# First stage of a hybrid layer on one core: loads reordered, c spread over all rows, squares and sums on four engines, sets that begin with 1, 2, 3 and 3 tiles of K

## The chip, the cores and the metric

The kernel runs on one core of a Trainium2 chip. A core has five engines that run beside each other, each with its own instruction queue that is worked off in order: TensorE (PE in the profile, with PEld for its weight loads), VectorE (DVE), ScalarE (ACT), GpSimd (POOL) and SyncE (SP), which here only starts DMA transfers. The metric is the device time of the whole program in microseconds; the median of three runs before is 2272.33 us (2261.13 to 2316.85).

## The reference

One layer over 256 positions of width 2048: a feed-forward block, a mixer of a convolution branch and a retention branch, a second feed-forward block, and a last norm. Every sub-layer's norm is scaled and shifted by vectors that are computed from a conditioning vector c. The change is in the first feed-forward block alone, and in what has to be there before it:

```python
c_act = jax.nn.silu(c)
mod = c_act @ ada_w[l] + ada_b[l]                  # 9 vectors of 2048
sh1, sc1, g1, ... = jnp.split(mod, N_MOD_LAYER, axis=-1)
h = modulate(rms_norm(x, ffn1_norm[l]), sh1, sc1)  # h * (1 + sc1) + sh1
x = x + HALF_STEP * g1[:, None, :] * swiglu(h, ffn1_w1[l], ffn1_w3[l], ffn1_w2[l])
```

with `swiglu(h, w1, w3, w2) = (silu(h @ w1) * (h @ w3)) @ w2` and a hidden width of 5632, which is 44 tiles of 128.

## The kernel before, in words

All activations are held transposed: 128 rows of a feature tile by 256 positions; x is 16 such tiles (K tiles). Weights are float32 in DRAM. Every weight tile is loaded into one of four buffers called `raw` (RAW = 4), is rounded to a high half `hi` by ScalarE (L190) and its rest `lo` is taken by VectorE (L193); the activations are split in the same way into `h[k][:, 0]` and `h[k][:, 1]`. A product of one weight block with one activation tile is then three matmuls, hi·hi, hi·lo and lo·hi, each 128x128 by 128x256 with its own weight load (L203, L204, L205).

**The start.** c is loaded as one row; four matmuls with a column of ones over that single row spread it over 128 rows (L86), and Silu makes `cb` of it (L87). x is loaded in four pieces of 512 KB. ScalarE squares x two tiles at a time and VectorE adds the squares up into `ssq`; two matmuls with ones sum over the rows (L264), and `rstd_from` makes r = 1/rms of it with one ScalarE step and four VectorE steps (L253 to L257).

**The modulation vectors** are not products on TensorE. A 1 MB tile of the transposed `ada_w` is loaded into a `raw` buffer, and one VectorE instruction multiplies it by `cb` and sums along the row (`ada_reduce`, L111). For each K tile of the first block two are needed: (1, k), the scale, and (0, k), the shift. `modulated` then makes `h[k]` from x, r, scale and shift (L329 to L340).

**The first stage** makes 24 of the 44 hidden tiles. They are 4 sets of 6; a set is 6 pairs of w1 and w3 blocks, one pair in one PSUM bank (there are 8 banks). A *unit* is one set and one K tile: one 768 KB load (`w13s`), 12 blocks, 36 matmuls, in `across`. There are 64 units. Since not all K tiles are there at the beginning, K is cut into four groups (KGROUPS = 3, 4, 4, 5 tiles); the sets are gone through forwards in one group and backwards in the next, and when a set's piece of K is done its six banks are put away: the first piece is copied to `part` by ScalarE (L443), later ones are added to it by VectorE (L445). So two sets that follow on from a group to the next stay in their banks.

**The order** of the modulation work is set by `unlock`: the 32 half steps (scale, then shift and `modulated`, of each K tile) are put ahead of the unit that needs them, or earlier at a PACE of 0.5 half steps a unit. Within these sequences a scheduler orders the instructions of each engine ahead of the run, by its own estimates; `ada_reduce` keeps its place in the program's order. On the chip the order on an engine is fixed, and an instruction that waits holds back all behind it.

Of the kernel before, what the change touches and what calls it, by code (L numbers as in the profile page):

```python
# [14 lines left out]
P = 128  # L15
# [15 lines left out]
KGROUPS = [3, 4, 4, 5]  # L31
PACE = 0.5
# [21 lines left out]
def hybrid_layer(ctx, tc, xT, c, vecs, rope, decay, adaT, w13, w13s, w13t, mixs, w2g, w_ab, w_qk, w_v, w_g,  # L54
# [20 lines left out]
    nc.sync.dma_start(vec, vecs)  # L75
    x = sb(keep, [P, ND, T], "x1", tag="x")
    x_away = dram.tile([P, ND, T], F32, name="x_away")
    for t in range(0, ND, 4):
        nc.sync.dma_start(x[:, t:t + 4], xT[:, t:t + 4])
    ones = sb(keep, [P, P], "ones")  # L80
    V.memset(ones, 1.0)
    cb = sb(keep, [P, D], "cb")
    for n in range(0, D, 1024):
        for u in range(n, n + 1024, 512):
            ps = bank("cb_ps")
            PE.matmul(ps, ones[0:1, :], crow[:, u:u + 512], start=True, stop=True)  # L86
            A.activation(cb[:, u:u + 512], ps, AF.Silu)  # L87
# [12 lines left out]

    def raw_load(src, n):
        r = wp.tile([P, 2048], F32, name="raw", tag="raw", bufs=RAW)
        nc.sync.dma_start(r[:, :n], src)
        return r

    def ada_load(j, t):
        return raw_load(adaT[(j * ND + t) * P:(j * ND + t + 1) * P, :], D)
# [71 lines left out]
    def prep(src, nk, w, ticks=True):  # L179
# [5 lines left out]
        for k0 in range(0, nk, hk):  # L185
# [4 lines left out]
            A.copy(hi[:, :c1 - c0], r[:, c0:c1])  # L190
# [42 lines left out]
    eps = sb(keep, [P, 1], "eps")  # L233
    V.memset(eps, EPS)
# [3 lines left out]
    def table(f, seen):  # L238

        A.activation(idle, seen, f, bias=eps[:, 0:1], scale=0.0)  # L240

    def warm(n, mv):

        ps = bank("warm")
        for i in range(n):
            PE.matmul(ps[:, 0:P], ones, mv[:, 0:P], start=True, stop=True, skip_group_check=True)

    def rstd_from(sums, n, name):
# [4 lines left out]
        A.activation(y, sums, AF.Abs_reciprocal_sqrt, bias=eps[:, 0:1], scale=1.0 / n)  # L253
        V.tensor_scalar(w, sums, -0.5 / n, -0.5 * EPS, op0=ALU.mult, op1=ALU.add)
        V.tensor_tensor(w, w, y, op=ALU.mult)
        V.tensor_tensor(w, w, y, op=ALU.mult)
        V.scalar_tensor_tensor(out=r, in0=w, scalar=1.5, in1=y, op0=ALU.add, op1=ALU.mult)  # L257
        return r
# [140 lines left out]
    with tc.tile_pool(name="ffn1", bufs=1) as pool:  # L399
        hh = new_h()  # L400
        for t in range(0, ND, 2):
            squares(pool, t, "s2", GROUPS[0] + 1)
        first = ada_load(1, 0), ada_load(0, 0)
        ada_reduce(1, 0, first[0])
        r = rstd_from(partition_sums([ssq[:, 0], ssq[:, 1]], "r0"), D, "r0")
        h = [hh[:, t] for t in range(ND)]

        def unlock(half):
            t = half // 2
            if t == 0:  # L410
                if half:
                    modulated(pool, hh, t, r, 0, 0, lambda: ada_reduce(0, 0, first[1]))
# [11 lines left out]
        k0 = 0  # L424
        for g, n in enumerate(KGROUPS):
            units += [(st, k) for st in (range(SETS) if g % 2 == 0 else reversed(range(SETS))) for k in range(k0, k0 + n)]
            k0 += n
        for i, (st, k) in enumerate(units):
            due += PACE if locked and locked[0] >= 2 * KGROUPS[0] else 0.0
            while locked and (locked[0] <= 2 * k + 1 or due >= 1.0):  # L430
                due = max(0.0, due - 1.0)
                unlock(locked.pop(0))
            begins = i == 0 or units[i - 1][0] != st
# [3 lines left out]
            across(prep(w13s[st, k], 2 * S0, P, False), h[k], banks, begins, ends)  # L437
# [362 lines left out]
```

## Time and profile before

| | |
|---|---|
| median of three runs | 2272.33 us (2261.13, 2272.33, 2316.85) |
| the profiled execution | 2286.55 us, of which its span is 2284.8 |
| PE busy | 2250.0 us (98%) in 19088 matmuls |
| DVE, ACT, POOL busy | 1765.1 us (77%), 1061.7 us (46%), 0.6 us |
| DMA | 616.86 MB, mean 270 GB/s |
| last matmul of the first stage ends at | 294.59 us |

Busy times are sums over the span. The first stage is 64 units of 36 matmuls; 40 us of it hold some 356 matmuls when TensorE has no gap. A row of the timeline or of the chain begins with its start in us from the span's start and its duration; the bracket at the end gives the idle time ahead of it and what ended that.

### The profile page before, as it was taken

What the parts mean: (1) busy time and instruction counts of PE and PEld (TensorE: products, weight loads), DVE (VectorE), ACT (ScalarE), POOL (GpSimd) and SP (SyncE); (2) the same over time, 40 slices, a digit from 0 to 9 for tenths busy, and PEclk for the clock granted to TensorE, in tenths of its full rate; (3) what the DMA queues carried; (4) which work ended last, traced back from release to release, by engine and by line L of the source; (5) the groups of instructions that cost most, each with busy time, mean ns of one, the idle gap of its engine ahead of it and who ended that gap; (6) DMA issues with size and microseconds to landing.
All of it is one profiled execution on the core that took longest, in us unless ns stands there. A gap on an engine that the chain in (4) does not pass through costs nothing.

```text
span 2284.8 us, 44660 instructions
## 1 busy us (share of the span) xinstructions
PE 2250.0 (98%) x19088; PEld 2224.5 (97%) x19088; DVE 1765.1 (77%) x2221; ACT 1061.7 (46%) x1360; POOL 0.6 (0%) x8
## 2 busy tenths in 40 slices
PE   7999999999999999999999999999999999999997
PEld 5999999999999999999999999999999999999997
DVE  7899887787778669898998788887766666666665
ACT  5544653334444644445544644445544443344443
POOL 0000000000000000000000000000000000000000
PEclk9999999999999999999999999999999999999999
DMA  9989689998888566555777688986877777777662
GB/s 338 356 319 337 219 291 324 341 341 319 323 311 328 171 218 206 172 169 183 248 267 268 229 320 326 355 291 227 296 260 257 270 255 267 272 276 265 251 247 85
DMA packets 92217, 616.86 MB, mean 270 GB/s; under 512 B 10225, under 2 KB 10481, under 8 KB 34673
## 3 DMA queue, kind: packets, MB, share of 16 engines
q1 hardware_dynamic: 90290, 609.81, 74.2%
q10 hardware_dynamic: 1728, 4.20, 0.5%
q8 instruction: 149, 2.44, 0.4%
q14 instruction: 50, 0.41, 0.0%
HBM read 609.77 MB, written 4.19 MB: 269 GB/s over the span
## 4 chain that ended last, share of the span: by engine, by line
PE 95%; DMA 2%; DVE 2%; ACT 1%; issue 1%; SPq 0%; DVEq 0%; ACTq 0%
PE ps L218 50%; PE ps L220 25%; PE ps L203 6%; PE ps L204 6%; PE ps L205 6%; DMA raw<-in_w13s 1%; DMA raw<-in_adaT 1%; DVE raw L111 0%; DVE lo L193 0%; DMA x<-in_xT 0%; DVE f L702 0%; ACT hi L190 0%; PE gn_v L264 0%; PE gn_m L264 0%; ACT part L443 0%
## 5 line engine op out<-in xcount | busy, mean ns | idle before, releaser
L190 ACT CAST hi<-raw 128x1024 fp32r<-128x1024 f32 (+2 forms) x864 | 843.8, 986 | 1101.7 <-PE ps L218 585.8
L193 DVE TENSOR_TENSOR lo<-raw,hi 128x1024 fp32r<-128x1024 f32 (+2 forms) x864 | 978.9, 1142 | 435.8 <-ACT hi L190 424.7
L218 PE MATMUL ps<-h,hi 128*128 128x256 f32 x5888 | 733.5, 277 | 0.0
L218 PEld LDWEIGHTS ps<-h,hi 128*128 128x128 f32 x5888 | 700.3, 188 | 0.2
L111 DVE CUSTOM_DVE_ANT_0 raw<-raw,cb,vec 128x2048 f32<-128x2048 f32 x176 | 412.8, 2345 | 6.2 <-DMA raw<-in_adaT 6.2
L220 PE MATMUL ps<-h,lo 128*128 128x256 f32 x2944 | 396.5, 277 | 0.0
L220 PEld LDWEIGHTS ps<-h,lo 128*128 128x128 f32 x2944 | 363.6, 188 | 0.0
L218 PE MATMUL ps<-s,hi 128*128 128x256 f32 x2816 | 357.4, 279 | 0.0
L218 PEld LDWEIGHTS ps<-s,hi 128*128 128x128 f32 x2816 | 339.8, 188 | 0.1
L204 PE MATMUL ps<-h,hi 128*128 128x256 f32 x1152 | 318.1, 279 | 4.0 <-DVE h L336 4.0
L203 PE MATMUL ps<-h,hi 128*128 128x256 f32 x1152 | 313.3, 279 | 8.6 <-ACT h L333 7.4
L205 PE MATMUL ps<-h,lo 128*128 128x256 f32 x1152 | 315.3, 278 | 0.0
L203 PEld LDWEIGHTS ps<-h,hi 128*128 128x128 f32 x1152 | 214.9, 189 | 10.1 <-ACT h L333 8.5
L204 PEld LDWEIGHTS ps<-h,hi 128*128 128x128 f32 x1152 | 218.0, 189 | 4.7 <-DVE h L336 4.5
L205 PEld LDWEIGHTS ps<-h,lo 128*128 128x128 f32 x1152 | 215.7, 189 | 0.0
L220 PE MATMUL ps<-s,lo 128*128 128x256 f32 x1408 | 193.9, 279 | 0.0
L220 PEld LDWEIGHTS ps<-s,lo 128*128 128x128 f32 x1408 | 176.6, 188 | 0.0
L472 DVE SCALAR_TENSOR_TENSOR acc<-y,vec,acc 128x256 f32<-128x256 f32 x240 | 114.0, 480 | 2.7
L218 PE MATMUL ps<-mg,hi 128*128 128x256 f32 x512 | 63.8, 276 | 0.0
L218 PE MATMUL ps<-r,hi 128*128 128x256 f32 x512 | 63.6, 276 | 0.0
L218 PEld LDWEIGHTS ps<-mg,hi 128*128 128x128 f32 x512 | 60.6, 188 | 0.1
L218 PEld LDWEIGHTS ps<-r,hi 128*128 128x128 f32 x512 | 60.5, 188 | 0.0
(161 smaller groups left out, 1183.4 us busy)
## 6 DMA issues: line engine op xcount, KB each, us to landing
raw<-in_adaT SPq DMA_DIRECT2D x176, 1024.0 KB, 6.0
raw<-in_w SPq DMA_DIRECT2D x148, 1024.0 KB, 5.6
raw<-in_w SPq DMA_DIRECT2D x64, 896.0 KB, 5.2
raw<-in_w13s SPq DMA_DIRECT2D x64, 768.0 KB, 6.3
raw<-in_w_v SPq DMA_DIRECT2D x16, 1024.0 KB, 4.9
raw<-in_w_g SPq DMA_DIRECT2D x16, 1024.0 KB, 4.9
raw<-in_w_gr SPq DMA_DIRECT2D x16, 1024.0 KB, 5.0
raw<-in_w_o SPq DMA_DIRECT2D x16, 1024.0 KB, 5.5
```

Source lines behind the costliest of these rows:

```text
L111: tc.keep_in_program_order(V.tensor_tensor_reduce(r, r, cb, 1.0, vec[:, b:b + 1], op0=ALU.mult, op1=ALU.add, accum_out=mod[:, j, t:t + 1]))
L190: A.copy(hi[:, :c1 - c0], r[:, c0:c1])
L193: V.tensor_tensor(lo[:, :c1 - c0], r[:, c0:c1], hi[:, :c1 - c0].bitcast(F32), op=ALU.subtract)
L203: PE.matmul(o, st[0], mv[0], start=start, stop=False, skip_group_check=skip)
L204: PE.matmul(o, st[0], mv[1], start=False, stop=False, skip_group_check=skip)
L205: PE.matmul(o, st[1], mv[0], start=False, stop=stop, skip_group_check=skip)
L218: PE.matmul(o, w[k][0], mv[k][:, half], start=k == 0 and half == 0, stop=False)
L220: PE.matmul(o, w[k][1], mv[k][:, 0], start=False, stop=k == n - 1)
L472: tc.keep_in_program_order(V.scalar_tensor_tensor(out=acc[:, t], in0=y[:, t, k:k + T], scalar=vec[:, dw + k:dw + k + 1], in1=acc[:, t], op ...
```

## The change

Nothing is computed differently in the later stages, except that `across`, the products of one unit, is also used at the start of the mixer and of the second block (16 units each), and is written in another order there too.

- **Loads.** The first `ada_w` tile (scale of K tile 0) is issued ahead of `vec` and x on SP; the second (shift of K tile 0) right behind x. c goes out on ScalarE's queue.
- **c.** It is loaded into row 0 of a tile of 128 rows that VectorE and GpSimd have set to zero, and the four matmuls now run over all 128 rows. Seven more warming matmuls (`warm`) stand ahead of them.
- **Squares and sums.** The eight squares of x go to ScalarE (six) and VectorE (two); three pairs are joined by an addition (two on VectorE, one on GpSimd), and TensorE sums what is left: five tiles of 128x512, ten matmuls in place of two. Of r's steps, one goes from VectorE to ScalarE and the other four to GpSimd. The ACT table for the root is loaded by a dummy step right behind the last square.
- **The first unit** (`prep_first`): its hi halves are taken ahead of the modulation of K tile 0, its lo halves behind it.
- **Products of a unit** (`across`): six blocks hi·hi, the same six hi·lo, then lo·hi, and then the other six blocks; before, the three matmuls of one block stood together.
- **K cuts.** The groups' ends now differ by set (KCUTS): the first group has 1, 2, 3 and 3 tiles of K in sets 0 to 3. PACE is 0.7.

```diff
-KGROUPS = [3, 4, 4, 5]
-PACE = 0.5
+KCUTS = [[0, 1, 6, 10, 16], [0, 2, 6, 11, 16], [0, 3, 6, 11, 16], [0, 3, 5, 11, 16]]
+PACE = 0.7
...
-    crow = sb(keep, [1, D], "crow", tag="h")
-    nc.sync.dma_start(crow, c)
...
+    V.memset(c0[:, :D // 2], 0.0)
+    nc.gpsimd.memset(c0[:, D // 2:], 0.0)
...
+    first = [ada_load(1, 0)]
+    nc.scalar.dma_start(c0[0:1, :], c)
+    vec = sb(keep, [P, V_ALL], "vec")
+    pin(nc.sync.dma_start(vec, vecs))
...
+    for t in range(0, ND, 4):
+        pin(nc.sync.dma_start(x[:, t:t + 4], xT[:, t:t + 4]))
+    first.append(ada_load(0, 0))
...
+    def cb_part(u):
+
+        ps = bank("cb_ps")
+        PE.matmul(ps, ones, c0[:, u * 512:(u + 1) * 512], start=True, stop=True)
+        pin(A.activation(cb[:, u * 512:(u + 1) * 512], ps, AF.Silu))
...
+        if V is nc.gpsimd:
+            A.activation(w, sums, AF.Identity, bias=eps[:, 1:2], scale=-0.5 / n)
...
     def across(w, h, banks, start, stop):
-        for b in range(2 * S0):
-            o = banks[b // 2][:, b % 2 * T:(b % 2 + 1) * T]
-            mm3(o, w[b], (h[:, 0], h[:, 1]), start and b % 2 == 0, stop, skip=True)
+        for b0 in range(0, 2 * S0, S0):
+            for half in range(3):
+                for b in range(b0, b0 + S0):
+                    PE.matmul(banks[b // 2][:, b % 2 * T:(b % 2 + 1) * T], w[b][half // 2], h[:, half % 2],
+                              start=start and b % 2 == 0 and half == 0, stop=stop and half == 2, skip_group_check=True)
...
+        warm(WARM[0] + 3, ones)
+        for u in range(3):
+            cb_part(u)
+        square(0, A)
+        square(1, V)
+        cb_part(3)
+        join(0, V)
+        square(2, A)
+        square(3, A)
+        join(2, nc.gpsimd)
         ada_reduce(1, 0, first[0])
-        r = rstd_from(partition_sums([ssq[:, 0], ssq[:, 1]], "r0"), D, "r0")
+        square(4, A)
+        square(5, V)
+        join(4, V)
+        square(6, A)
+        square(7, A)
+        pin(table(AF.Abs_reciprocal_sqrt, sq[7][:, 0, 0:1]))
+        for i in (0, 2, 4, 6, 7):
+            total(i)
+        ada_reduce(0, 0, first[1])
+        r = rstd_from(ps, D, "r0", nc.gpsimd)
+        warm(WARM[0], sq[7][:, 0])
...
-            due += PACE if locked and locked[0] >= 2 * KGROUPS[0] else 0.0
-            while locked and (locked[0] <= 2 * k + 1 or due >= 1.0):
+            while i and locked and (locked[0] <= 2 * k + 1 or due >= 1.0):
                 due = max(0.0, due - 1.0)
                 unlock(locked.pop(0))
+            due += PACE if i > 1 else 1.0
```

What the scheduler makes of it on VectorE, where K tile 0 is made: `ISA raw` is `ada_reduce`, `xr`, `hf` and `h` are the steps of `modulated`, `lo` the rest of a weight half. Before:

```order
L257 SCALAR_TENSOR_TENSOR r0_r_135<-r0_w_134,r0_y_133 128x256
L329 TENSOR_TENSOR xr_141<-x1_70,r0_r_135 128x256
L111 ISA raw_126,mod_91<-raw_126,cb_78,vec_68 128x2048
L111 ISA mod_91 128x1
L329 TENSOR_TENSOR xr_211<-x1_70,r0_r_135 128x256
L193 TENSOR_TENSOR lo_160<-raw_154,hi_158 128x768
L193 TENSOR_TENSOR lo_166<-raw_154,hi_164 128x768
L335 TENSOR_SCALAR hf_145<-xr_141,scale_93,mod_91 128x256
L111 ISA raw_204,mod_91<-raw_204,cb_78,vec_68 128x2048
L111 ISA mod_91 128x1
L336 TENSOR_TENSOR h_101<-hf_145,h_101 128x256
```

The same place in the changed program:

```order
L445 TENSOR_TENSOR sq_102<-sq_102,sq_103 128x512
L128 ISA raw_86,mod_89<-raw_86,cb_88,vec_78 128x2048
L128 ISA mod_89 128x1
L347 TENSOR_TENSOR xr_184<-x1_80,r0_r_154 128x256
L347 TENSOR_TENSOR xr_299<-x1_80,r0_r_154 128x256
L353 TENSOR_SCALAR hf_187<-xr_184,scale_91,mod_89 128x256
L354 TENSOR_TENSOR h_97<-hf_187,h_97 128x256
L386 TENSOR_TENSOR lo_178<-raw_172,hi_176 128x768
L386 TENSOR_TENSOR lo_183<-raw_172,hi_181 128x768
```

The shift's reduce has moved ahead of r, and the reduce for K tile 1 that stood between `hf` and `h` is gone from there.

A second place on VectorE, further on: where a set's second piece of K has ended (before, set 2 behind the 20th unit; `part` are the six additions) and the following units' `lo` come. Before:

```order
L193 TENSOR_TENSOR lo_1255<-raw_1247,hi_1253 128x768
L445 TENSOR_TENSOR part_649<-ps_1033,part_649 128x512
L111 ISA raw_1293,mod_91<-raw_1293,cb_78,vec_68 128x2048
L111 ISA mod_91 128x1
L445 TENSOR_TENSOR part_651<-ps_1034,part_651 128x512
L445 TENSOR_TENSOR part_653<-ps_1035,part_653 128x512
L445 TENSOR_TENSOR part_655<-ps_1036,part_655 128x512
L445 TENSOR_TENSOR part_657<-ps_1037,part_657 128x512
L445 TENSOR_TENSOR part_659<-ps_1038,part_659 128x512
L193 TENSOR_TENSOR lo_1301<-raw_1297,hi_1299 128x768
```

In the changed program, set 1 behind the 18th unit; `lo_1187` and `lo_1191` are the 19th unit's, `lo_1241` the 20th's:

```order
L517 TENSOR_TENSOR part_353<-ps_966,part_353 128x512
L517 TENSOR_TENSOR part_355<-ps_967,part_355 128x512
L212 TENSOR_TENSOR lo_1191<-raw_1183,hi_1189 128x768
L517 TENSOR_TENSOR part_357<-ps_968,part_357 128x512
L128 ISA raw_1229,mod_89<-raw_1229,cb_88,vec_78 128x2048
L128 ISA mod_89 128x1
L517 TENSOR_TENSOR part_359<-ps_969,part_359 128x512
L517 TENSOR_TENSOR part_361<-ps_970,part_361 128x512
L128 ISA raw_1173,mod_89<-raw_1173,cb_88,vec_78 128x2048
L128 ISA mod_89 128x1
L212 TENSOR_TENSOR lo_1241<-raw_1237,hi_1239 128x768
```

One reduce stood among the additions there before; now there are two.

More of the change, by code (lines that the diff above doesn't have):

```diff
@@ L99, in hybrid_layer @@
     set_apart = set()
[L101 to L107, printed above, removed]
     def ada_reduce(j, t, r):
@@ L238, in table, with rstd_from @@
     def table(f, seen):
[L240 to L248, printed above, removed]
+        return A.activation(idle, seen, f, bias=eps[:, 0:1], scale=0.0)
+    def rstd_from(sums, n, name, V=V):
         y = sb(keep, [P, T], name + "_y", tag="rs_y")
@@ L436, in hybrid_layer @@
                 banks = [bank() for _ in range(S0)]
-            across(prep(w13s[st, k], 2 * S0, P, False), h[k], banks, begins, ends)
+            if i:
+                w = ahead.pop() if ahead else prep(w13s[st, k], 2 * S0, P, False)
+            else:
+                w = prep_first(w13s[0, 0], lambda: [unlock(locked.pop(0)) for _ in range(2)])
+                ahead = [prep(w13s[units[1]], 2 * S0, P, False, True)]
+            across(w, h[k], banks, begins, ends)
             for b in range(S0 if ends else 0):
```

81 lines of the change are left out of this document (58 added, 23 removed).

## The prediction

> **What bounds the kernel now.** I read the page's totals first, then the busy time by stretches of the first stage, then the chain of waits at the start, then the timeline of single engines where TensorE stands still.
>
> ```profile
> PE 2250.0 (98%) x19088; PEld 2224.5 (97%) x19088; DVE 1765.1 (77%) x2221; ACT 1061.7 (46%) x1360; POOL 0.6 (0%) x8
> ```
>
> TensorE is the bound of the whole, so the change can win only where TensorE stands still in the first 295 us. The next rows show where that is (columns: stretch, its length, then busy us and count of PE, PEld, DVE, ACT, POOL, then granted clock, DMA share, GB/s).
>
> ```profile
> 0.00:10.00 10.00, 7.16 (x8) 2.49 (x8) 1.75 (x5) 5.05 (x9) 0.39 (x6) 1.00 0.78 259
> 10.00:20.00 10.00, 2.08 (x4) 1.18 (x4) 9.17 (x14) 5.98 (x9) 0.00 (x0) 1.00 1.01 422
> 20.00:30.00 10.00, 5.69 (x26) 5.40 (x27) 10.00 (x15) 2.77 (x4) 0.00 (x0) 1.00 0.91 321
> 30.00:40.00 10.00, 8.57 (x71) 8.00 (x70) 9.96 (x15) 5.11 (x8) 0.00 (x0) 1.00 0.90 326
> 40.00:80.00 40.00, 40.00 (x356) 40.00 (x354) 32.56 (x39) 25.81 (x41) 0.00 (x0) 1.00 0.92 347
> 80.00:120.00 40.00, 38.97 (x344) 38.77 (x343) 36.33 (x46) 21.82 (x32) 0.00 (x0) 1.00 0.91 344
> 120.00:160.00 40.00, 40.00 (x356) 40.00 (x355) 36.87 (x48) 18.76 (x26) 0.00 (x0) 1.00 0.93 341
> 160.00:200.00 40.00, 40.00 (x356) 40.00 (x355) 39.07 (x53) 17.60 (x24) 0.00 (x0) 1.00 0.89 318
> 240.00:280.00 40.00, 40.00 (x342) 40.00 (x341) 32.35 (x55) 23.20 (x43) 0.00 (x0) 1.00 0.60 198
> ```
>
> From 40 us on TensorE is full, 356 matmuls in 40 us, which is 0.113 us each when those that only reach into the window are left out. A unit of 36 is 4.1 us. Only 1.0 us is missing, between 80 and 120. The loss is the start. What else stands there matters as much: VectorE is busy for 33 to 39 us of each 40, and the DMA engines for about 0.9 of the time. There is little room to feed TensorE faster than it now eats. (The last row has 342 matmuls at the same granted clock, 4% fewer; this execution has such a slower stretch, which the change doesn't touch.)
>
> The chain that ended last, and the timeline of PE in the start:
>
> ```profile
> 2.96 8.07 DMA x<-in_xT
> 13.74 2.09 PE r L264 x4
> 15.85 0.48 ACT r_y L253
> 17.74 0.44 DVE r_r L257
> 18.54 2.34 DVE raw L111
> 21.23 1.74 DVE lo L193 x2
> ```
> ```profile
> 2.48 7.16 PE L86 MATMUL cb_ps<-crow,ones 1*128 1x512 f32 x8 [2.48 <-DMA crow<-in_c]
> 21.58 1.65 PE L203 MATMUL ps<-h,hi 128*128 128x256 f32 x6 [5.77 <-ACT h L333]
> 25.95 0.58 PE L204 MATMUL ps<-h,hi 128*128 128x256 f32 x1 [2.72 <-DVE h L336]
> 26.76 0.41 PE L204 MATMUL ps<-h,hi 128*128 128x256 f32 x1
> 26.97 0.41 PE L205 MATMUL ps<-h,lo 128*128 128x256 f32 x1
> 29.53 0.28 PE L205 MATMUL ps<-h,lo 128*128 128x256 f32 x1
> 29.65 0.28 PE L203 MATMUL ps<-h,hi 128*128 128x256 f32 x1
> 38.05 0.39 PE L204 MATMUL ps<-h,hi 128*128 128x256 f32 x1
> 942.01 1.02 PE L264 MATMUL gn_m<-gn_a,ones 128*128 128x256 f32 x4
> ```
>
> x has landed at 11.03 (call that moment T), r is there at 18.2, and the first product starts at 21.58. TensorE runs without a gap only from 38.05, when 78 products are out. The 180th, the end of five units, is out at 38.05 + 102 x 0.113 = 49.6. I compare at that point.
>
> **The change part by part.** I count from T and from r.
>
> *T.* 1.05 MB of `ada_w` now lies ahead of x; at the 422 GB/s of 10 to 20 us that is 2.5 us, so T = 13.5. Below that it could be 12.0, if the first transfers are slow whatever they are (259 GB/s in the first 10 us). c on ScalarE's queue waits for the zeroing of its tile, some 1 us, and `cb` is needed only at T - 2.4: covered.
>
> *r.* The squares cost ScalarE and VectorE less than before, but VectorE's second join now stands behind the reduce of the first `ada_w` tile. First piece of x at T - 3.7 (1.24 us a piece at 422), square and join 1.3, reduce 2.3, square and join 1.2: T + 1.1. Behind it TensorE still has three of five pairs of sums. A pair is four rows of the trace: 1.02 at 942 us, 2.09 at 13.74, at half speed. One-row products did not raise the speed in 7 us (2.48: eight in 7.16); products of 128 rows did after 3.4 us (0.21 apart at 26, 0.12 from 29.53). With c over 128 rows and seven warming products TensorE is at work from 1 us on, so I take full speed: 2.8 us, T + 4.0. At half speed it is 2.6 more.
>
> The Trainium skill, TensorE: Matmul & The Clock Gate, Part 1, says that the gate opens after some 3.4 us of busy time and shuts after an idle window of that length. The 3.4 us agree with 25.95 to 29.53; that it looks at busy time alone does not agree with the eight one-row products. By it the first unit begins at half speed after the pause ahead of it, and if it didn't the sum would be 1.7 us lower.
>
> Then 0.48 for the root and about the same for the step that goes to ScalarE, and four steps on GpSimd, of which no row has the like. These two are the nearest:
>
> ```profile
> 0.73 0.11 POOL L97 MEMSET apart_w<- 128x16 f32 x1 [0.29 <-POOLq L790]
> 0.78 0.14 POOL L97 MEMSET apart_s<- 128x48 f32 x1
> ```
>
> 32 elements more cost 0.03 us: 0.9 ns each, so 256 elements of two inputs come to 0.48 + 0.1, say 0.6; the lower end is VectorE's own 0.44 (17.74), the upper 0.11/16 x 256 = 1.8. Four steps: 1.8 to 7.0, and I take 2.4, since the slope is GpSimd's own. r is at T + 7.4 = 20.9, later than the 18.2 of before by 2.7 (range 0 to 8).
>
> The Trainium skill, GPSIMD Engine Reference, Performance versus the Vector engine, gives two-input steps on GpSimd 1.96 times VectorE's time, against this move; as an estimate by that, four steps are 3.4 us and the sum 1.0 higher.
>
> *The first units.* Here the new order wins. Before, two reduces of 2.34 and two `lo` lay between r and the second half of `h`, which held TensorE until 25.95 and twice more until 38.05. Now `xr` and ScalarE's step follow r at once: first product at r + 1.0, and the rest of `h` is there long before its 12 products. Unit 0 has 16 products at half speed and 20 at full, to r + 6.7; unit 1 follows without a wait, to r + 10.8.
>
> ```profile
> L190 ACT CAST hi<-raw 128x768 fp32r<-128x768 f32 x8 | 6.3, 832 | 10.1 <-DMA raw<-in_w13s 10.1
> L443 ACT COPY part<-ps 128x512 f32<-128x512 f32 x2 | 1.2, 589 | 0.4 <-PE ps L205 0.4
> ```
>
> But set 0 is put away after one unit: five copies (0.57 each, overlapped) and the `hi` of unit 2 (1.5), a copy, then unit 3's first `hi`, at r + 12.5: 1.7 us of wait. ScalarE's `h` of K tile 1 comes behind the other half, at 13.8: 0.4. Its rest on VectorE stands behind three reduces and six `lo`, at 16.8: 0.7. So five units are out at r + 25.9 = 46.8, against 49.6: **2.8 us won**, and the 1.0 us of waiting at 91 us is of an arrangement that is gone: **1.0 won**.
>
> *The rest of the ramp.* PACE 0.7 and the new cuts bring the 32 reduces in by unit 42, where before there were 27. VectorE's costs a step:
>
> ```profile
> L193 DVE TENSOR_TENSOR lo<-raw,hi 128x768 fp32r<-128x768 f32 x99 | 91.3, 952 | 10.8 <-ACT hi L190 10.2
> L111 DVE CUSTOM_DVE_ANT_0 raw<-raw,cb,vec 128x2048 f32<-128x2048 f32 x26 | 61.0, 2347 | 6.2 <-DMA raw<-in_adaT 6.2
> L445 DVE TENSOR_TENSOR part<-ps,part 128x512 f32<-128x512 f32 x36 | 23.3, 681 | 0.6 <-PE ps L205 0.6
> ```
>
> Steps in a row overlap by some 0.08, so a `lo` costs 0.87, a reduce 2.27, an addition 0.60, the small ones 0.34. Between the `lo` of unit 10 and of unit 42 the new program has 64 `lo`, 22 reduces, 30 additions and 21 small steps (and 11 of 0.07): 55.7 + 49.9 + 18.0 + 7.9 = 131.5 us, for 32 units that TensorE does in 32 x 36 x 0.113 = 130.2. Before, with 17 reduces, it was 119. VectorE becomes as slow as TensorE, and any hold on it now reaches TensorE. The hold is where a set's second piece is put away, as the program of before shows it:
>
> ```profile
> 109.05 0.69 DVE L445 TENSOR_TENSOR part<-ps,part 128x512 f32<-128x512 f32 x1 [0.60 <-PE ps L205]
> 109.66 2.34 DVE L111 CUSTOM_DVE_ANT_0 raw<-raw,cb,vec 128x2048 f32<-128x2048 f32 x1
> 111.93 3.08 DVE L445 TENSOR_TENSOR part<-ps,part 128x512 f32<-128x512 f32 x5
> 114.92 0.94 DVE L193 TENSOR_TENSOR lo<-raw,hi 128x768 fp32r<-128x768 f32 x1
> ```
>
> VectorE waits there for the set's last products, works off six additions and a reduce, and only then the next `lo`. In the new order behind unit 17, the first addition can start some 2.3 us ahead of the unit's end E; then six additions, two reduces and three `lo` halves end at E - 2.3 + 3.6 + 4.5 + 2.6 = E + 8.4. TensorE has unit 18 and 24 products of the next, 6.8 us, so it waits about 1.7 to 2. The same stands behind unit 31 (two reduces around the `lo` of the unit after next). Two such places: **4 us lost** (0 if VectorE is ahead by more, 8 if all five such places hold).
>
> *Loads.* From unit 5 to unit 42, 37 x 0.786 + 26 x 1.049 = 56.4 MB; in 151 us of products that is 373 GB/s, where 347 was the most in 40 us, with four buffers at
>
> ```profile
> raw<-in_w13s SPq DMA_DIRECT2D x25, 768.0 KB, 6.4
> raw<-in_adaT SPq DMA_DIRECT2D x19, 1024.0 KB, 7.0
> ```
>
> from issue to landing. 422 shows that the engines can do more when requests lie ready. At 350 they need 161 us, which is what the waits above and a lead of some 3 us leave: **1 us lost** (0 to 8).
>
> *Behind unit 42* only 0.786 MB a unit and no reduces are left, 192 GB/s: nothing waits, as from 240 to 280 us before. `across` in two later stages issues the same matmuls; the orders of before (three on one block, and long runs on one block) both show 0.113, so I cost it at nothing.
>
> Sum against the profiled execution: 2286.6 - 2.8 - 1.0 + 4 + 1 = 2287.8. That execution lies 14 us above the median of 2272.3; the same +1.2 there gives 2273.
>
> **The rivals.**
>
> 1. *The gain stays* (VectorE and the loads keep up, the pieces fall where TensorE has reserves). For it: VectorE did 39.07 of 40 us between 160 and 200 without a gap on PE. Against it: it was paced by TensorE there. -3.8, and up to -7 if the three early waits are shorter too: 2267.
> 2. *The loads become the bound*, and it is slower than before: four buffers are held longest when VectorE has no reserve, and each transfer needs 6 to 7 us. It decides if the mean from unit 5 to unit 42 stays below 350 GB/s. At 341, the figure of 120 to 160 us, 165 us are needed, 14 over the products and 11 over the lead: 2272 - 3.8 + 11 = 2279; at 330 it is 2285. Against it: between 40 and 80 the DMA share was 0.92, with some room.
> 3. *r comes late:* sums at half speed (+2.6) or GpSimd steps near their upper end (+4.6), with no cover, as all products wait for r: 2277. The Trainium skill, GPSIMD Engine Reference, Specifications, says that GpSimd shares its SBUF interface with VectorE's two-input steps, which speaks for this one; the second reduce (2.34) ends about where GpSimd's steps begin.
> 4. *The order of products changes their rate,* or the scheduler's new order does: 3456 products, 0.004 us apart either way as the two rates in the stretches are: 14 us up or down. No row speaks for it.
>
> **How the numbers follow.** Forecast 0.38, rivals 0.25, 0.22, 0.10 and 0.05. Cases reach from -7 to +13 around 2272, and the runs of before themselves from 2261 to 2287; 2252 to 2292 takes in about 8 of 10. A measurement of this kernel tells 2%, 45 us, from no change; no case above reaches that, and only the unknown rest is left: 0.02 faster, 0.95 the same, 0.03 slower.
>
> **What would show it.** Right: x landed at 13 to 14 us, r near 21, first product near 22 and no gap in unit 0; the 180th product at 46 to 48; gaps on PE in front of `lo` products near 105 and 160 us, with VectorE at 39 of 40 us in 70 to 200; end of the stage at 293 to 297. Wrong: a full PE from 45 us on (rival 1), ScalarE's `hi` waiting for `w13s` all through with PE behind it (2), r after 23 (3).

## The result, and the profile after

| | before | changed |
|---|---|---|
| median, six runs each | 2270.55 us (2261.13 to 2316.85) | 2297.58 us (2292.97 to 2305.03) |
| ratio | | 1.0101, 95% interval 1.0056 to 1.0145 |
| profiled execution | 2286.55 us, span 2284.8 | 2292.97 us, span 2291.2 |

The changed kernel is slower, by 1.0%: less than 2%, but the interval does not hold 1. The forecast of 2273 (2252 to 2292) missed it. (The run of 2316.85 us was in a slower state of the chip and is not in the ratio.)

Two views of the changed kernel, the page's totals and the busy time by stretches (columns as in the prediction):

```profile
PE 2250.6 (98%) x19126; PEld 2222.0 (97%) x19126; DVE 1762.8 (77%) x2216; ACT 1056.4 (46%) x1360; POOL 6.9 (0%) x14
```
```profile
20.00:30.00 10.00, 5.52 (x26) 4.61 (x25) 3.21 (x7) 4.08 (x7) 3.02 (x4) 0.84 0.39 135
30.00:40.00 10.00, 9.32 (x69) 9.13 (x68) 9.97 (x14) 6.03 (x11) 0.00 (x0) 0.84 0.77 259
40.00:80.00 40.00, 37.35 (x324) 36.73 (x323) 34.42 (x43) 22.09 (x38) 0.00 (x0) 1.00 0.96 358
80.00:120.00 40.00, 38.37 (x339) 38.17 (x338) 37.41 (x50) 18.17 (x27) 0.00 (x0) 1.00 0.87 314
120.00:160.00 40.00, 38.91 (x333) 38.71 (x332) 37.74 (x49) 19.45 (x28) 0.00 (x0) 1.00 0.94 359
160.00:200.00 40.00, 37.91 (x317) 36.81 (x317) 37.21 (x49) 15.20 (x22) 0.00 (x0) 1.00 0.86 336
240.00:280.00 40.00, 40.00 (x355) 40.00 (x354) 33.08 (x56) 25.19 (x45) 0.00 (x0) 1.00 0.58 189
```

Totals hide it: busy time is what it was. Between 20 and 30 us VectorE works for 3.2 us where it worked for 10.0, and the loads move 135 GB/s where they moved 321. From 40 to 200 TensorE is short of work in every row, where before it was full but for 1.0 us. From 240 on it is full again.

How late each point of the first stage is, read off the starts of the products: the 180th ends five units, the 1512th ends unit 41. In some stretches products come 0.118 us apart and not 0.1133 (the prediction's last window row shows one). They fall differently in every execution, so a column gives what the stage lost to them (the time between neighbouring products over 0.1133, gaps left out), and the next the stage's end without it.

| kernel | first product | 180th out | unit 42 begins | stage ends | of it slower products | end without them | ratio to before |
|---|---|---|---|---|---|---|---|
| before | 21.6 | 49.7 | 202.0 | 294.4 | 2.8 | 291.6 | 1 |
| changed | 28.9 | 54.5 | 217.4 | 307.3 | 2.2 | 305.1 | 1.0101 |
| changed, again | 29.2 | 55.2 | 220.1 | 310.0 | 2.1 | 307.9 | 1.0111 (1.0065 to 1.0157) |
| before + new order of products | 21.1 | 49.0 | 200.0 | 289.7 | 0.0 | 289.7 | 1.0018 (0.9981 to 1.0055) |
| before + new cuts, PACE 0.7 | 20.7 | 46.1 | 210.2 | 299.9 | 2.0 | 297.9 | one run |
| before + order + cuts, PACE 0.5 | 21.0 | 46.5 | 202.3 | 293.1 | 1.3 | 291.8 | 1.0022 (0.9982 to 1.0062) |
| changed, old cuts and PACE | 28.5 | 63.3 | 214.2 | 304.0 | 0.2 | 303.8 | 1.0063 (1.0022 to 1.0103) |
| changed, PACE 0.5 | 28.7 | 54.0 | 210.9 | 303.9 | 2.9 | 301.0 | 1.0085 (1.0051 to 1.0119) |
| changed, squares first | 24.0 | 49.5 | 215.1 | 304.9 | 2.6 | 302.3 | one run |
| changed, squares first, joins on VectorE | 23.8 | 50.2 | 217.0 | 310.4 | 6.4 | 304.0 | 1.0086 (1.0040 to 1.0131) |
| changed, start mended, PACE 0.5 | 23.9 | 53.7 | 208.2 | 299.7 | 0.2 | 299.5 | 1.0020 (0.9984 to 1.0056) |

The stage ends 13.5 and 16.3 us later in the two profiles: 4.8 and 5.5 us are lost up to the 180th product, 8.6 and 10.9 from there to unit 42, nothing behind it (89.9 us for the last 22 units in both, against 89.8 before, slower products taken off). Behind the stage the products from the 6504th on take the same time within 1 us, slower products again taken off; the 4200 ahead of them are spoken of under the sum. The two profiles of the one kernel differ by 2.8 us at the stage's end, so a difference of that size between single profiles says little.

Where the start went, by the timeline of the changed kernel, engine by engine (L111 spreads c, L112 is Silu of it, L442 squares, L445 joins, L449 sums over the rows, L264 to L273 make r, L347 and L351 begin `h`):

```profile
6.70 6.63 PE L111 MATMUL cb_ps<-c,ones 128*128 128x512 f32 x8 [2.30 <-DMA c<-in_c]
18.94 4.54 PE L449 MATMUL r<-sq,ones 128*128 128x256 f32 x12 [0.29 <-DVE sq L445]
28.86 4.62 PE L370 MATMUL ps<-h,hi 128*128 128x256 f32 x24 [4.48 <-ACT h L351]
...
12.20 0.60 ACT L112 ACTIVATE cb<-cb_ps 128x512 f32<-128x512 f32 x1 [1.11 <-PE cb_ps L111]
12.69 0.62 ACT L442 ACTIVATE sq<-x 128x512 f32<-128x512 f32 x1
...
15.09 2.38 POOL L445 TENSOR_TENSOR sq<-sq 128x512 f32<-128x512 f32 x1 [13.29 <-ACT sq L442]
24.44 0.72 POOL L269 TENSOR_TENSOR r_w<-r_w,r_y 128x256 f32<-128x256 f32 x1 [6.97 <-ACT r_w L266]
26.06 0.85 POOL L272 TENSOR_SCALAR r_w<-r_w 128x256 f32<-128x256 f32 x1
26.99 0.72 POOL L273 TENSOR_TENSOR r_r<-r_w,r_y 128x256 f32<-128x256 f32 x1
...
8.06 0.69 DVE L442 TENSOR_TENSOR sq<-x 128x512 f32<-128x512 f32 x1 [5.98 <-DMA x<-in_xT]
14.00 2.35 DVE L128 CUSTOM_DVE_ANT_0 raw<-raw,cb,vec 128x2048 f32<-128x2048 f32 x1
18.20 0.69 DVE L445 TENSOR_TENSOR sq<-sq 128x512 f32<-128x512 f32 x1
27.75 0.76 DVE L347 TENSOR_TENSOR xr<-x,r_r 128x256 f32<-128x256 f32 x2 [6.59 <-POOL r_r L273]
```

VectorE squares its part of the first piece of x at 8.06, when it lands; ScalarE begins its own at 12.69. It stands behind three pieces of `cb`, and each of these waits for products that come 1.7 us apart. VectorE's first join, which needs that square, ends at 14.03. The chain of work that ended last goes another way to the same moment:

```profile
2.18 4.39 DMA c<-in_c
6.70 6.65 PE cb_ps L111 x8
13.37 0.61 ACT cb L112
14.00 2.35 DVE raw L128
16.40 1.09 DVE scale L137
...
18.94 4.56 PE r L449 x12
```

c lands at 6.6, and the last piece of `cb` is there at 13.97. VectorE's first reduce needs all of `cb`, and in VectorE's order it stands ahead of the last square and the last join. So `cb` holds r in two ways, through ScalarE's queue and through that reduce, and both end at 14.0. From there on it adds up: the last join begins at 18.2, the sums end at 23.5, r is there at 27.7. Until then four buffers hold two tiles of `ada_w` and two units that nobody can work off, which is the 135 GB/s.

### The profile page after: what moved, and what is told of

It reads as the page before. It is cut to its first block, busy times and chain, and to the rows that moved or that the text cites. A ratio compares the mean times of both kernels' runs of the same rounds, so it can differ in the third digit from the quotient of the medians.

```text
span 2291.2 us, 44737 instructions
## 1 busy us (share of the span) xinstructions
PE 2250.6 (98%) x19126; PEld 2222.0 (97%) x19126; DVE 1762.8 (77%) x2216; ACT 1056.4 (46%) x1360; POOL 6.9 (0%) x14
## 4 chain that ended last, share of the span: by engine, by line
PE 92%; DVE 3%; DMA 3%; issue 1%; ACT 1%; POOL 0%; DVEq 0%; ACTq 0%
PE ps L237 49%; PE ps L239 24%; PE ps L370 14%; DMA raw<-in_w13s 2%; PE ps L223 2%; PE ps L224 2%; PE ps L222 2%; DMA raw<-in_w 1%; DVE raw L128 1%; DVE lo L212 1%; DVE part L517 0%; ACT hi L207 0%; PE cb_ps L111 0%; DVE f L774 0%; PE r L449 0%
## 5 line engine op out<-in xcount | busy, mean ns | idle before, releaser
L237 PE MATMUL ps<-h,hi 128*128 128x256 f32 x5888 | 732.4, 277 | 0.5 <-ACT hi L207 0.5
L237 PEld LDWEIGHTS ps<-h,hi 128*128 128x128 f32 x5888 | 699.5, 188 | 0.8 <-ACT hi L207 0.7
L239 PE MATMUL ps<-h,lo 128*128 128x256 f32 x2944 | 395.8, 277 | 0.0
L239 PEld LDWEIGHTS ps<-h,lo 128*128 128x128 f32 x2944 | 363.0, 188 | 0.0
L370 PE MATMUL ps<-h,hi 128*128 128x256 f32 x2304 | 299.7, 278 | 12.1 <-ACT h L351 6.2
L370 PEld LDWEIGHTS ps<-h,hi 128*128 128x128 f32 x2304 | 279.7, 189 | 14.7 <-ACT hi L207 7.7
L370 PE MATMUL ps<-h,lo 128*128 128x256 f32 x1152 | 165.7, 277 | 3.3 <-DVE lo L212 3.3
L370 PEld LDWEIGHTS ps<-h,lo 128*128 128x128 f32 x1152 | 146.6, 188 | 4.2 <-DVE lo L212 4.0
L223 PE MATMUL ps<-lo,h 128*128 128x512 f32 x128 | 50.8, 397 | 0.0
L222 PE MATMUL ps<-hi,h 128*128 128x512 f32 x128 | 50.6, 395 | 0.0
```

The source lines that it names most:

```text
L222: PE.matmul(o, st[0], mv[0], start=start, stop=False, skip_group_check=skip)
L223: PE.matmul(o, st[0], mv[1], start=False, stop=False, skip_group_check=skip)
L237: PE.matmul(o, w[k][0], mv[k][:, half], start=k == 0 and half == 0, stop=False)
L239: PE.matmul(o, w[k][1], mv[k][:, 0], start=False, stop=k == n - 1)
L370: PE.matmul(banks[b // 2][:, b % 2 * T:(b % 2 + 1) * T], w[b][half // 2], h[:, half % 2], start=start and b % 2 == 0 and half == 0, stop=s ...
```

## The experiments

Two theories stood against each other for the start (D: ScalarE's squares are held by `cb`; E: GpSimd is the cause), and several for the ramp, the stretch from the 180th product to unit 42 (F: VectorE's work bounds it; G: only the late start does; H: the loads do; C and J: the places where sets end; I: the start leaves reduces over).

**The changed kernel again, and the order of products alone.** The second is the kernel before with one edit:

```diff
-        for b in range(2 * S0):
-            o = banks[b // 2][:, b % 2 * T:(b % 2 + 1) * T]
-            mm3(o, w[b], (h[:, 0], h[:, 1]), start and b % 2 == 0, stop, skip=True)
+        for b0 in range(0, 2 * S0, S0):
+            for half in range(3):
+                for b in range(b0, b0 + S0):
+                    PE.matmul(...)
```

> The changed kernel once more, unaltered, for a second profile. In the two profiles so far the first stage ends 12.9 us later (307.3 against 294.4) and everything behind it is alike but for stretches in which products come 4% slower; the medians differ by 27 us. Theory A (the loss is the first stage's alone, and the slow stretches fall by chance): stage end again near 307, the time 13 to 15 us over the kernel before, a ratio near 1.006. Rival B (the change costs some 14 us more somewhere behind the first stage, by its order of products or by longer slow stretches): ratio near 1.012 again, and the new profile shows the slow stretch longer than the 240 us of the first one.

> The kernel before with one part of the change: the order of products in across (six blocks side by side, by halves). Theory A: products stay 0.1133 us apart and nothing waits, ratio 1.000 (2268 to 2274 where the kernel before has 2271). Rival B (the order changes the rate of products, or the scheduler's order around them): 14 us more, ratio 1.006, with products of across more than 0.1133 us apart, in all three places where across is called.

The loss repeats: 1.0111, with the stage's end at 310.0. Slower products took 10.8 us of the whole span this time (13.4 in the first profile), so rival B's longer stretch is not what the new profile shows; but the ratio is B's and not A's, and I come back to that.

The order alone costs nothing in the stage. These are stretches of that kernel:

```profile
80.00:120.00 40.00, 40.00 (x356) 40.00 (x355) 37.67 (x49) 22.49 (x35) 0.00 (x0) 1.00 0.92 352
160.00:200.00 40.00, 40.00 (x356) 40.00 (x355) 39.05 (x52) 17.88 (x24) 0.00 (x0) 1.00 0.86 307
```

356 products in 40 us, as before, and the 1.0 us of waiting at 91 us is gone. Its ratio, 1.0018, holds 1.

**Cuts and pace.** Four kernels: the changed one with `PACE = 0.5`; the same with the old cuts besides (`KCUTS = [[0, 3, 7, 11, 16]] * 4`); the kernel before with the new `KCUTS`, `PACE = 0.7` and the `due` lines of the change; and the last with the new order and `PACE = 0.5`.

> The changed kernel with PACE 0.5 in place of 0.7 and its own cuts. Theory A (the number of reduces in the ramp makes VectorE the bound): most of the ramp's 8 us comes back, stage end near 300, 6 us over the kernel before. Rival C (the cuts do it: where sets end, VectorE holds six additions and TensorE waits, whatever the pace): gaps stay behind units 14, 17, 27, 31 and 36, stage end at 304 or later. A third possibility: the reduces that the pace leaves are forced in a row at the last group's first tiles (two for one unit near unit 41), with a gap of 2 to 4 us there.

> The changed kernel with the sets of before (every set 3, 4, 4 and 5 tiles of K) and PACE 0.5, so that the new start and the new order of products are left. Theory A: the start stays late (first product near 28.9, the 180th out near 52 to 55 against 49.7), and behind it the gaps in the ramp are gone, since VectorE has 17 reduces and not 22 between units 10 and 42: stage end near 298 to 300, 5 us over the kernel before, ratio 1.002. Rival (the late start itself leaves the loads without reserve for the whole ramp): gaps remain to unit 42 and the stage ends past 303, ratio 1.004 or more.

> The kernel before with only the cuts and PACE 0.7 of the change: old loads, old start, old order of products. Theory F (with 0.7 reduces a unit VectorE cannot keep up, whatever the start): first product at 21 to 22 as before, the 180th near 46, and then gaps of 6 to 12 us up to unit 42; stage end at 296 to 300 with products at 0.1133. Rival I (the ramp of the changed kernel suffers from its start: VectorE idle for 6 us while it waits for r, and reduces left over): gaps in the ramp under 3 us, stage end at 289 to 291.

> The kernel before with the new cuts and the new order of products, but PACE 0.5: old loads, squares and sums. Theory F: at 0.5 there are 27 reduces by unit 42 as in the kernel before, which VectorE managed with 3 to 6 us in hand; the shorter first sets bring the 180th product to about 46, and gaps in the ramp are 0 to 3 us: stage end at 287 to 290, where the kernel before has 291.6 without its slow stretch; ratio 0.998 to 1.000, not to be told from 1. Rival J (the new cuts themselves make VectorE late, through the additions where sets end, as the run with PACE 0.5 has still 6 us of gaps): gaps of 4 to 7 us, stage end at 292 to 295, ratio 1.001 to 1.002.

The third separates best. On the old start the new cuts do what they say: five units are out at 46.1 and not 49.7. Then the ramp takes it back and more: 162 us without slower products from the 180th to the 1512th, against 152 before. What TensorE waited for there, in the whole of its start and ramp:

```profile
PE ps L205 <- DVE lo L193: 7.6, 5, 3.6
PE ps L203 <- ACT h L333: 5.8, 1, 5.8
PE ps L204 <- DVE h L336: 2.3, 1, 2.3
PE ps L203 <- ACT hi L190: 0.5, 1, 0.5
```

(Columns: waited for, us in total, times, longest.) The second and third are the start. The 7.6 us for `lo` are the ramp, so what F forecast is there on a start that is not late, and rival I falls. But the places where sets end have their part in it: the two longest of these waits, 3.2 and 3.6 us, are in units 19 and 33, each the second unit behind the end of a piece of set 1. With PACE 0.5 neither kernel with the new cuts waits in these two units, so it takes the cuts and the higher pace together. The ramp then costs 5.9 us of gaps in the changed kernel, where most of 9.9 was to come back, and 3.6 on the old start: less, as F has it, but not the 0 to 3 that I wrote. The shorter first sets bring 2.5 us by the 180th product (46.5 against 49.0 with the old cuts and the same order of products) and lose them by unit 42 (202.3 against 200.0). Rival J is nearer there.

The old cuts on the new start lose nothing in the ramp at all: 151.0 us, which is 1332 products without a gap. But they lose 14.3 us up to the 180th product (63.3, against 49.0 for the same cuts and order on the old start; I expected 52 to 55). Six reduces are due before unit 2, and VectorE, which has done two of them at 21.3, stands idle until r comes at 27.4. That start is bad with either set of cuts, and the new cuts hide 9 us of it.

**The start.** First the squares ahead of the pieces of `cb` and VectorE's first reduce behind its last join, two moves in one edit (shown below, against the changed kernel); then all joins on VectorE besides (seven, two pairs of sums left); then also r's steps on VectorE and the second reduce behind them, with PACE 0.5:

```diff
-        for u in range(3):
-            cb_part(u)
+        pin(table(AF.Silu, ones[:, 0:1]))
         square(0, A)
         square(1, V)
-        cb_part(3)
+        cb_part(0)
         join(0, V)
         square(2, A)
         square(3, A)
         join(2, nc.gpsimd)
-        ada_reduce(1, 0, first[0])
+        cb_part(1)
         square(4, A)
...
+        cb_part(2)
+        cb_part(3)
+        ada_reduce(1, 0, first[0])
```

> The changed kernel with ScalarE's squares of x ahead of the pieces of cb that they stood behind (and VectorE's reduce behind its last join); GpSimd's join and its four steps of r stay. Theory D (r is late because ScalarE does not square the first piece of x before 12.69 though it landed at 8.04: it is held by cb, whose products come 1.7 us apart): squares from 8.1 to 13.2, the sums of squares end near 19 where they ended at 23.5, r near 23 where it was 27.7, first product near 24. Rival E (GpSimd is the cause: its join of 2.38 us and four steps of 3.3 us): the sums wait for GpSimd's join as before and r stays at 26 or later.

> As the run with squares first, and further all joins on VectorE, seven in place of three, so that two pairs of sums are left of five; the four steps of r stay on GpSimd. Theory D: sums end near 16, r near 19.5, first product near 21, 8 us earlier than in the changed kernel. What follows in the ramp tells two readings apart. Theory F (the ramp is short of VectorE itself, with 32 reduces due by unit 42): VectorE is the pace and starts 8 us earlier, so the gaps of 10 us between units 5 and 42 stay at 6 to 10, and the stage ends at 298 to 300. Rival G (the late start had left the loads without reserve, four buffers held until VectorE came): with the start mended gaps fall under 3 us and the stage ends at 290 to 293, as early as that of before.

> The changed kernel with its start mended in full and PACE 0.5: squares ahead of cb, joins and the steps of r on VectorE, nothing of either on GpSimd, the reduce of the second tile of ada_w behind r as in the kernel before. Theory D and F: GpSimd's steps took 3.3 to 5.1 us (one of them waited 2.8 us for a reduce of VectorE's); on VectorE they take 1.3 to 1.7, r near 18.8, first product near 22, the 180th at 46 to 48; with 27 reduces by unit 42 gaps in the ramp of 2 to 6 us; stage end at 291 to 296, ratio 1.000 to 1.003, 8 to 12 us under the changed kernel. Rival G (late loads, not VectorE's work): stage end at 287 to 290.

With the squares first, rows of the timeline:

```profile
8.04 0.63 ACT L442 ACTIVATE sq<-x 128x512 f32<-128x512 f32 x1 [3.72 <-DMA x<-in_xT]
...
13.88 4.48 PE L449 MATMUL r<-sq,ones 128*128 128x256 f32 x20
24.00 5.49 PE L370 MATMUL ps<-h,hi 128*128 128x256 f32 x24 [4.75 <-ACT h L351]
...
11.76 1.27 POOL L445 TENSOR_TENSOR sq<-sq 128x512 f32<-128x512 f32 x1 [9.95 <-ACT sq L442]
```

Theory D: the first product comes at 24.0, 4.9 us earlier, with GpSimd's join and four steps where they were. The edit takes both of `cb`'s holds away, the one on the squares and the one on the reduce; no run takes away one alone, and by the trace of the changed kernel either would have held VectorE until 14.0. All joins on VectorE bring the first product only 0.2 us further, because of this (GpSimd's row, then VectorE's, of the second kernel):

```profile
18.13 2.78 POOL L270 TENSOR_TENSOR r_w<-r_w,r_y 128x256 f32<-128x256 f32 x1
...
18.00 2.34 DVE L128 CUSTOM_DVE_ANT_0 raw<-raw,cb,vec 128x2048 f32<-128x2048 f32 x1
```

The sums were done at 16, as expected, but the second of GpSimd's steps took 2.78 us where it takes 0.72 alone: it ended 0.6 us behind the reduce on VectorE. So theory E has a part too, of 2 us. With r's steps on VectorE the reduce stands behind them instead, and the first product is again at 23.9. Against my 22, the sums ended at 17.7 and not at 16; c landed 1.2 us later in that execution and its products began at 8.0, which is my reading of it, not a test. Behind a wait of 3 us for `hi`, from 38 to 41 us, TensorE ran at half speed for a while (granted clock 0.91 from 40 to 80), so that five units were out at 53.7 and the stage ended at 299.5, later than either reading had it.

What matters more is the rest of those rows of the table. In the first two kernels the 180th product is 4.3 to 5.7 us earlier; the stage's end is 302.3 and 304.0, against 305.1 and 307.9 in the two profiles of the changed kernel. So a part of the gain is lost again in the ramp, where the gaps are 12.5 and 13.4 us against 9.9 and 12.1; how large a part, single profiles do not tell. Rival G, with gaps under 3 us and an end at 290 to 293, is out.

**Work or bytes.** Two kernels that leave half of the sums out, one by the reduce and one by the load:

```diff
+        n = D // 2 if j < 2 and t else D
-        V.tensor_tensor_reduce(r, r, cb, ...)
+        V.tensor_tensor_reduce(r[:, :n], r[:, :n], cb[:, :n], ...)
```
```diff
+        n = D // 2 if j < 2 and t else D
-        return raw_load(adaT[(j * ND + t) * P:(j * ND + t + 1) * P, :], D)
+        return raw_load(adaT[(j * ND + t) * P:(j * ND + t + 1) * P, :n], n)
...
+        for _ in range(D // n):
+            V.tensor_tensor_reduce(r[:, :n], r[:, :n], cb[:, :n], ...)
```

> The changed kernel with every reduce of ada_w in the first stage but the first two done over 1024 of its 2048 columns: half of those sums is left out. All loads stay. Theory F (VectorE bounds the ramp): 30 x 1.15 = 35 us of VectorE's work go, gaps between units 5 and 42 fall from 10 to under 2 us, stage end near 297. Rival H (the loads bound the ramp): gaps stay at 6 or more, ScalarE's hi waits as long for w13s (79.5 us from 40 to 220).

> The changed kernel with only 1024 columns of each tile of ada_w loaded in the first stage (but the first two tiles), and the reduce of 1024 columns done twice: half of those sums is left out, VectorE's time stays (2 x 1.2 us for 2.35) and 15.7 MB of loads go. Theory F (VectorE bounds the ramp): gaps between units 5 and 42 stay at 6 to 12. Rival H (the loads bound it): gaps fall under 3, stage end near 298.

With half the reduce the gaps from the 180th product to unit 42 are 5.0 us (9.9 and 12.1 in the two profiles of the changed kernel), where F had them under 2; with half the load they are 18.2, where F had 6 to 12 and H under 3. The stage ends at 299.8 and 314.8. VectorE's groups from 55 to 215 us, of the first kernel and of the second:

```profile
L129 DVE CUSTOM_DVE_ANT_0 raw<-raw,cb,vec 128x1024 f32<-128x1024 f32 x25 | 31.9, 1280 | 1.9 <-DMA raw<-in_adaT 1.9
```
```profile
L131 DVE CUSTOM_DVE_ANT_0 raw<-raw,cb,vec 128x1024 f32<-128x1024 f32 x47 | 60.1, 1280 | 0.4 <-DMA raw<-in_adaT 0.4
```

Two halves cost VectorE 2.56 us for 2.35, 0.2 us more a tile: less to load, a little more to do, and TensorE waits longer. So the bytes are not the bound (H falls), and less work for VectorE helps (F). But F as I put it is not the whole of it. 5 us stay when VectorE's work there has shrunk by a fifth (22 of the ramp's reduces at 1.07 less, 24 of 131 us). And in the second kernel TensorE hardly waits for VectorE's `lo`; it waits for ScalarE's `hi` (55 to 215 us):

```profile
PE ps L373 <- ACT hi L210: 10.5, 13, 2.4
PE ps L373 <- ACT h L360: 1.5, 1, 1.5
PE ps L373 <- DVE lo L215: 0.3, 1, 0.3
```

ScalarE waits there for `w13s` (68.4 us in the same stretch), though the DMA engines move only 241 GB/s, since a load starts only when one of the four buffers is free: all but 3 us of the waits of the queue that starts the loads are for a step of VectorE. What bounds the ramp is then the round of the four buffers through VectorE's queue, in which VectorE's work is the largest part that was varied. A kernel with more buffers would tell work from buffers; there is no such run.

## Why the prediction was wrong

**T was right in sign, r was wrong.** x landed at 11.95 (13.5 was forecast). r was to be there at 20.9 and came at 27.7. The step that failed is the first one of *r*: I called `cb` "covered" and put it at nothing, and took each square as done when its piece had landed. `cb` was needed at T - 2.4, which is 9.6 by the measured T, and was complete at 13.97: c, from its new place in the queues, landed at 6.6 (2.5 before), and its eight products took 6.6 us. Of ScalarE's queue I had counted the squares but not the three pieces of `cb` ahead of them, which the order of its instructions shows. The last join was to end at T + 1.1, 13.1 by the measured T, and ended at 18.9, 5.8 us late: 4.4 by `cb`, 1 by a small VectorE step that GpSimd's join held up, the rest in the square and join. Next, the sums: 2.8 us at full speed were forecast and 4.54 measured, at a mean granted clock of 0.62 from 18.94 to 23.48; that is 1.7 of the 2.6 that I had priced for half speed. GpSimd's four steps were to take 2.4 and took 3.3 (24.44 to 27.71), inside the range of 1.8 to 7.0; the slope of a memset gave 0.6 a step, and the row says 0.72 for two inputs and 0.85 for the step with one. With 1.5 us won by the earlier T these are the 6.8 us. Rival 3, r late, with a chance of 0.10 and a price of 5 us, had its sign come true, r after 23; but its two causes, the sums and GpSimd's steps, brought 2.6 us together, and the 5.8 that count most were no rival's.

**The first units were right in their sum.** First product at r + 1.0: it was r + 1.2. Five units out at r + 25.9: they were at r + 26.8. The waits in between came to 3.2 us for 2.8, partly by luck: 0.8 for 1.7 ahead of unit 2, and in its second half 2.1 for 0.7, there for ScalarE's `hi`. The gain of 2.8 us failed by r alone. That the new cuts on the old start give 46.1, where the sum said 46.8, is no proof of it: r and the order of work are others there.

**The ramp: right mechanism, wrong size.** I had written VectorE's work from the `lo` of unit 10 to that of unit 42 as 131.5 us, and 119 before. The same stretches, changed and before:

```profile
76.00:219.30 143.30, 137.41 (x1169) 135.25 (x1169) 133.44 (x172) 63.06 (x93) 0.00 (x0) 1.00 0.90 336
```
```profile
68.60:199.40 130.80, 129.77 (x1145) 129.57 (x1144) 121.18 (x156) 63.13 (x89) 0.00 (x0) 1.00 0.91 335
```

133.4 and 121.2: the work was forecast to within 2.2 us. What I set against it was not. I compared 131.5 with TensorE's 130.2 and called it even, as if VectorE could be busy all the time. It stood idle for 9.6 us of such a stretch before, when TensorE set the pace, and for 9.9 now that TensorE waits for it. What it waited for now:

```profile
DVE part L517 <- PE ps L370: 3.7, 2, 2.0
DVE lo L212 <- ACT hi L207: 3.6, 9, 0.8
DVE raw L128 <- DMA raw<-in_adaT: 2.3, 4, 0.9
```

Part of it is the hold at set ends, which I had placed behind units 17 and 31. It is there, at both places, with 1.8 and 2.8 us of TensorE's waiting against the 1.7 to 2 forecast. The first of them, VectorE and then TensorE:

```profile
106.37 0.69 DVE L517 TENSOR_TENSOR part<-ps,part 128x512 f32<-128x512 f32 x1 [2.00 <-PE ps L370]
...
110.51 2.35 DVE L128 CUSTOM_DVE_ANT_0 raw<-raw,cb,vec 128x2048 f32<-128x2048 f32 x1
112.78 0.08 DVE L128 DVE_READ_ACCUMULATOR2_ANT mod<- 128x1 f32 x1
112.78 1.29 DVE L517 TENSOR_TENSOR part<-ps,part 128x512 f32<-128x512 f32 x2
113.97 2.35 DVE L128 CUSTOM_DVE_ANT_0 raw<-raw,cb,vec 128x2048 f32<-128x2048 f32 x1
...
116.24 3.56 DVE L212 TENSOR_TENSOR lo<-raw,hi 128x768 fp32r<-128x768 f32 x4
...
117.25 0.96 PE L370 MATMUL ps<-h,lo 128*128 128x256 f32 x6 [1.63 <-DVE lo L212]
```

The rest are small waits at other units, the longest of 0.7 to 1.3 us, all for ScalarE's `hi`. The term of 4 us lost was mis-sized: the holds took 4.6 in the first profile, and some 5 more were lost in these other waits, for which the sum had nothing but the 1 us of the loads. In all eleven profiles here with whole reduces VectorE is busy for 0.90 to 0.93 of this stretch and no more, so counting on the whole of its time was the error. Why it stays at that is not shown; with the reduces halved it is busy for 0.80, and TensorE still waits.

**The bytes and the order were right, the buffers were not.** 1 us was taken for the loads; halving the bytes of `ada_w` did not shorten the stage, so the bandwidth that rival 2 priced, with a chance of 0.22, was the wrong worry. Its test came true all the same: the mean from unit 5 to unit 42 is 338 GB/s, below its 350; but it is 335 in the kernel before, where TensorE does not wait. What I had named as its sign, ScalarE's `hi` waiting for `w13s` all through, is there in the changed kernel and less in the one before (40 to 220 us):

```profile
ACT hi L207 <- DMA raw<-in_w13s: 79.5, 29, 5.8
```
```profile
ACT hi L190 <- DMA raw<-in_w13s: 45.1, 20, 5.8
```

With fewer bytes the stage was no shorter, so ScalarE waits because buffers come free late, and VectorE frees them. That part of rival 2, four buffers held longest when VectorE has no reserve, is what the traces show. `across` at nothing was right: the stage ends 1.9 us earlier with it than without.

**Sum.** Forecast was +1.2 us; the stage alone, by the traces, is +13.5 and +16.3. The miss of 12 to 15 us is 8 up to the 180th product, nearly all of it r, and 5 to 7 in the ramp. The measured 27 us between the medians (23 by the ratio, 13 to 33 by its interval) is more. Slower products took 24 us of the span in the profile of before, 13.4 and 10.8 in those of the changed kernel, and between 1 and 26 in the others; where they are few, TensorE waits some 4 us more for ScalarE (`hi` and `s`) in the first block's later products, in the kernel before with the new order too (482.6 us without slower products for 4200 products, 478.5 in before, 482.3 and 484.7 in the changed kernel). They can account for the rest only if they lasted longer, on the average, in the changed kernel's other executions. The ratios of the two kernels that have the new order on the old start, 1.0018 and 1.0022, also lie above what their stages say, but hold 1. This stays open.

**A version that beats both** was not found. The order alone has the earliest end of the stage, 289.7, and cannot be told from the kernel before by its time.

## What to carry to other kernels

When two engines are near balance, do not compare one's work with the other's time: take from the trace what share of such a stretch the feeding engine is busy (here 0.90 to 0.93), and count only that. To start the bound engine earlier is worth less than it looks when the engine that feeds it has no reserve: the start here was made some 5 us faster, and the stage 1 to 6. And when steps are written in a new order, walk each engine's queue from its first instruction, and ask of each when its input is there: here three short Silus held a square for 4.6 us, and one reduce that needed the same late input stood ahead of the last join; no engine's busy time showed either.

## What the runs showed of the hardware

- **GpSimd and VectorE hold each other up.** GpSimd's join took 1.27 us with VectorE free and 2.38 beside a reduce; a step of 0.72 took 2.78. Both ended 0.6 to 1.1 us behind the reduce, as if they had waited for the whole of it. It goes the other way too: a VectorE step on one column, 0.15 us elsewhere, took 1.09 while that join ended (row below). The Trainium skill, GPSIMD Engine Reference, Specifications, says that the two share an SBUF interface. The trace agrees.

```profile
16.40 1.09 DVE L137 SCALAR_TENSOR_TENSOR scale<-mod,vec 128x1 f32<-128x1 f32 x1
```

- **Warming of 3.4 us is a matter of luck.** Fourteen warming rows kept TensorE busy from 1.05 to 4.4 us in all nine profiles that have them. In six the products of c, which came after a pause of 2.2 us or more, still began at half speed, 0.85 us apart (three pieces 1.7 us apart in the changed kernel). In the other three profiles the granted clock was full from 4.1, 4.4 and 4.7 us on, for 3.41 us; where c landed within that time (at 6.8 us, all joins on VectorE), its first products came 0.43 to 0.50 us apart. In these profiles the stretches of one clock in the start last 3.41 us or a multiple of it. The Trainium skill, TensorE: Matmul & The Clock Gate, Part 1, asks for some 3.4 us of busy time, in windows that run freely and do not begin with the kernel. The traces agree.
- **TensorE's slower stretches are its own.** Where products came 0.118 us apart, the granted clock still read 1.00, and VectorE's reduce (2.35 us) and ScalarE's `hi` took what they take elsewhere. What sets these stretches off was not found.
